# Five of 22 up-projection column pairs by seven block products, with one operand of the down-projection kept in DRAM meanwhile

## The chip, the cores and the metric

The kernel runs on one core of a Trainium2 chip. The metric is the device time of one launch in microseconds (us). TensorE (PE) multiplies, VectorE (DVE) and ScalarE (ACT) work elementwise, GpSimd (POOL) does small things, and SyncE (SP) issues nearly all DMAs. Each engine takes its instructions in the order in which they stand in its own list and stops at the first one whose inputs are not ready.

## The reference

One encoder block on 512 tokens of width 1024, in float32: two attention branches, then a gated feed-forward with a causal convolution of width 3 over the tokens. The change touches the feed-forward alone:

```python
def conv_glu(x, w_up, conv_w, conv_b, w_down):
    hid = x @ w_up                      # 512 x 1024 by 1024 x 5632
    hid = lax.conv_general_dilated(hid, ...) + conv_b
    gate, up = hid[..., :D_FF], hid[..., D_FF:]
    return (jax.nn.silu(gate) * up) @ w_down

x = x + conv_glu(rms_norm(x, norm2_g[l]), ...)
```

## The kernel before

**Products.** A float32 operand is split into hi and lo parts; every product is three matmuls (hi by hi, hi by lo, lo by hi). On the activations' side these are `hth` and `htl`, the transposed, normalised tokens (8 blocks of 128 features by 512 tokens).

**The up-projection.** The 5632 columns are worked through as 22 column pairs, up0 to up21: 128 gate columns and the 128 up columns that belong to them. A pair multiplies into two PSUM banks, `pg` and `pu`, with 8 blocks of features x 3 x 2 = 48 matmuls of 512 tokens. Only up0 and up1 run in halves of 256 tokens, since they start while the second half of the tokens is still being normalised.

**Around a pair.** `run_chunk` interleaves pair j with `split_gen` of pair j+1: ACT casts the raw weights to `whi`, DVE subtracts to get `wlo`, and SP then loads the raw weights of j+3 into the place that came free (1 MB a pair, two places). When `pg` is done, `conv` runs on it: one ACT activation for the last tap into `cg`, two DVE steps for the other taps, then SiLU on ACT. `pu` gets the same into `ub`, and DVE multiplies. `cg` has one place. `BANK` hands out PSUM banks in turn.

**For the down-projection,** which is done by seven block products already, `pair_sums` makes two operands from every second pair: `ax`, used in the first of its two sweeps, and `ay` (768 KB), used in the second. Before the change all eleven of each stay in SBUF.

**Order.** Nothing is queued dynamically: the order of each engine's list is fixed when the program is built, in part by the order of the Python generators and in part by the scheduler that merges them. The lists below are of the built programs.

Of the kernel before, what the change touches and what calls it, by code (L numbers as in the profile page):

```python
# [8 lines left out]
F32 = mybir.dt.float32  # L9
F32R = mybir.dt.float32r  # L10
AF = mybir.ActivationFunctionType
ALU = mybir.AluOpType
# [3 lines left out]
P = 128  # L16
# [42 lines left out]


CHUNKS = _chunks()


@with_exitstack
def block_kernel(ctx: ExitStack, tc: tile.TileContext, x, xt, params, g2, rbx, wts, wd0, wd1, out):
# [71 lines left out]
    def split_down(n, raw, hi, lo):  # L137
# [23 lines left out]
        else:  # L161
# [3 lines left out]
            yield  # L165
            part(0, raw[:, 0:1024])

    def split_gen(i, pieces):
# [6 lines left out]
        sh = 48 if key[:2] in ("qA", "kA", "vA", "vB") else 16 if key in ("up0", "up1") else 0  # L175
        n = 512 * kn if i >= FIRST_DN else 2048
        hi = wp.tile([P, 2112], F32R, tag="whi", name=f"whi_{key}")[:, sh:sh + n]
        lo = wp.tile([P, 2112], F32R, tag="wlo", name=f"wlo_{key}")[:, sh:sh + n]
        splits[key] = (hi.rearrange("p (k c) -> p k c", k=kn), lo.rearrange("p (k c) -> p k c", k=kn))
        if i >= FIRST_DN:  # L180
            yield from split_down(i - FIRST_DN, raw, hi, lo)
        n = 2048 // pieces
        for j in range(pieces if i < FIRST_DN else 0):
            sl = slice(n * j, n * (j + 1))
            if i == 0 and j == 0:
                V.tensor_copy(hi[:, sl], raw[:, sl])
            else:
                A.copy(hi[:, sl], raw[:, sl])  # L188
            E = G if i == 2 else V
            E.tensor_tensor(lo[:, sl], raw[:, sl], hi[:, sl].bitcast(F32), op=ALU.subtract)  # L190
            if j < pieces - 1:
                yield


        nxt = {0: None, 1: i + 3, 2: None}.get(i - FIRST_DN, i + 2)
        if nxt is not None and nxt < len(order):
            next(load(nxt))
        yield

    pos = {k: i for i, k in enumerate(order)}  # L200

    def run_chunk(key, body, pieces=4):

        sp = split_gen(pos[key] + 1, pieces)
        hi, lo = splits.pop(key)
        for _ in body(hi, lo):
            next(sp, None)
            yield
        for _ in sp:
            pass  # L210
# [11 lines left out]

    pp = ctx.enter_context(tc.tile_pool(name="pp", bufs=1, space=PSUM))
    dram = ctx.enter_context(tc.tile_pool(name="dram", bufs=1, space=bass.MemoryType.DRAM))


    reset = pool_c.tile([P, S], F32, tag="reset", name="reset")
# [35 lines left out]
    def norm_T(src, xn, gain, t, psum, nm):  # L263

        ss = pool_c.tile([P, 1], F32, tag="ss", name=f"ss_{nm}{t}", bufs=4)
        dump = pool_st.tile([P, D], F32, tag="skh", name=f"dump_{nm}{t}", bufs=2)
        A.activation(dump, src, AF.Square, accum_out=ss)
        rs = rstd_of(ss, 1, D, f"rs_{nm}{t}")
        for b in range(2):
            cs = slice(b * 512, (b + 1) * 512)  # L270
            V.scalar_tensor_tensor(xn[:, cs], src[:, cs], rs[:, 0:1], gain[b], op0=ALU.mult, op1=ALU.mult)
            ps = psum(f"tp_{nm}{t}{b}")
            for k in range(4):
                PE.transpose(ps[:, k * P:(k + 1) * P], xn[:, (4 * b + k) * P:(4 * b + k + 1) * P], ident)
            p3 = ps.rearrange("p (k q) -> p k q", k=4)
            hv = hth[:, 4 * b:4 * b + 4, t * P:(t + 1) * P]
            A.copy(hv, p3)
            V.tensor_tensor(htl[:, 4 * b:4 * b + 4, t * P:(t + 1) * P], p3, hv.bitcast(F32), op=ALU.subtract)

# [531 lines left out]
    def up_mm(ps, hi, lo, o, c0, c1):  # L811
        for k in range(NK):
            mm3(ps[:, c0:c1], hi[:, k, o:o + P], lo[:, k, o:o + P],
                hth[:, k, c0:c1], htl[:, k, c0:c1], k == 0, k == NK - 1)
            if k == 3:
                yield
        yield

    def gate(j, pg):
        g = fp.tile([P, S], F32, tag="cg", name=f"cg{j}", bufs=1)  # L820
        conv(pg, j, g)
        A.activation(g, g, AF.Silu)
        return g

    def pair_sums(i):

        u0, u1 = ub[:, 2 * i % 4, :], ub[:, 2 * i % 4 + 1, :]
        u = ub[:, 2 * i % 4:2 * i % 4 + 2, :].rearrange("p a b -> p (a b)")
        lo_, hi_ = slice(0, 256), slice(256, 512)
        t = {}  # L830
        if i < 8:
            ax = fp.tile([P, 2048], F32R, tag="ax", name=f"ax{i}", bufs=8)
            ay = fp.tile([P, 1536], F32R, tag="ay", name=f"ay{i}", bufs=8)
        else:

            pool = fp if i == 8 else late["hp"]
            ax = pool.tile([P, 2048], F32R, tag=f"ax{i}", name=f"ax{i}")
            ay = pool.tile([P, 1536], F32R, tag=f"ay{i}", name=f"ay{i}")
            if i == 8:
                keep[0] = fp.tile([P, S], F32, tag="t2", name="t2_0")  # L840
        pairs[i] = (ax, ay)

        def sums():
            t["st"] = st = fp.tile([P, 768], F32, tag="st", name=f"st{i}", bufs=1)
            s1, s42 = st[:, 0:256], st[:, 256:768]
            if i == 9:

                s42 = fp.tile([P, S], F32, tag="cg", name="s42_9", bufs=1)
            s4, s2 = s42[:, 0:256], s42[:, 256:512]
            t["s42"] = s42  # L850
            ins = [V.tensor_tensor(s1, u0[:, hi_], u1[:, hi_], op=ALU.add),
                   V.tensor_tensor(u0[:, hi_], u0[:, lo_], u0[:, hi_], op=ALU.subtract),
                   V.tensor_tensor(s2, s1, u0[:, lo_], op=ALU.subtract),
                   V.tensor_tensor(s4, u1[:, lo_], s2, op=ALU.subtract)]
            return ins

        def halves(a, parts):
            ins, n = [], a.shape[-1] // 2
            for o, src in parts:
                sl = slice(o, o + src.shape[-1])  # L860
                A.copy(a[:, sl], src)
                ins.append(V.tensor_tensor(a[:, n + o:n + sl.stop], src, a[:, sl].bitcast(F32), op=ALU.subtract))
# [13 lines left out]
    def up_fin(j, pg, pu, g=None):  # L876
        if g is None:
            g = gate(j, pg)
        u = ub[:, j % 4, :]
        conv(pu, NF + j, u)  # L880
        late["fin"] = (V.tensor_tensor(u, g, u, op=ALU.mult),)
        if j % 2 == 1 and j // 2 < 9:
            for step in pair_sums(j // 2):
                step()

    def up_body(j):
        def body(hi, lo):
            pg, pu = BANK(f"pg{j}", j - 1), BANK(f"pu{j}", j - 1)
            yield from up_mm(pg, hi, lo, 0, 0, S)
            g = gate(j, pg)  # L890
            yield from up_mm(pu, hi, lo, P, 0, S)
            up_fin(j, pg, pu, g)
        return body


# [2 lines left out]
    def up_first(j):  # L898
        def body(hi, lo):
            pg, pu = BANK(f"pg{j}", 0), BANK(f"pu{j}", 0)  # L900
            halves.append((hi, lo, pg, pu))
            yield from up_mm(pg, hi, lo, 0, 0, 256)
            yield from up_mm(pu, hi, lo, P, 0, 256)
            if j == 1:
                for i, (h, l, g, u) in enumerate(halves):
# [3 lines left out]
        return body  # L909

    for j in range(NF):
        for _ in run_chunk(f"up{j}", up_first(j) if j < 2 else up_body(j), pieces=4 if j < 2 else 2):
            pass

# [147 lines left out]
def _layout(inputs):  # L1062
# [12 lines left out]
    for i, (_, kn, parts) in enumerate(CHUNKS[:-2 * NP]):  # L1075
        views = [f[name][0][r0:r0 + kn * P, c0:c0 + n] for name, r0, c0, n in parts]
        w = views[0] if len(views) == 1 else np.concatenate(views, axis=1)
        wts[i] = w.reshape(kn, P, 2048 // kn).transpose(1, 0, 2).reshape(P, 2048)

    w = f["w_ffn_down"][0].reshape(NP, 2, P, 2, 512)  # L1080
# [20 lines left out]
```

## Time and profile before

| | us |
|---|---|
| median of 3 runs (lowest, highest) | 731.25 (730.97, 731.89) |
| profiled execution, and its span | 730.74, 729.0 |
| TensorE busy in the span | 723.3 |
| up2 starts | 401.70 |
| down-projection starts | 619.30 |
| DVE busy, ACT busy in the span | 533.8, 380.4 |

The span is what the profiler sees of the execution; 1.7 us lie around it. Times inside the program are counted from the span's start. In lines of the profile an instruction is named by its line, engine, output and inputs, with tile numbers left out; the first number is its start, the second its duration. Neighbouring instructions of one engine overlap, so that what one costs is read from start to start.

### The profile page before, as it was taken

The page shows a single profiled execution, that of the slowest core. Times are in us where ns is not written, and L with a number is a line of the kernel's source. Part 1 is how long each engine was busy: PE and PEld are TensorE (multiplying, and loading weights), DVE is VectorE, ACT ScalarE, POOL GpSimd, SP SyncE. Part 2 cuts the span into 40 slices and gives each one's busy share as a digit, 9 for nine tenths or more (in the row PEclk, how much of TensorE's full clock was granted, in tenths as well). Part 3 has the DMA queues.
Part 4 walks back from the last instruction along what each step waited for, and adds up shares of the span by engine and source line. Part 5 has one row for each costly group of instructions (what it writes and reads, how often), then busy time and mean ns, then how long its engine had stood idle before and what let it go on. Part 6 is the DMA issues. An engine that isn't in the chain of part 4 may idle for free.

```text
span 729.0 us, 10033 instructions
## 1 busy us (share of the span) xinstructions
PE 723.3 (99%) x3839; PEld 623.0 (85%) x3839; DVE 533.8 (73%) x967; ACT 380.4 (52%) x685; POOL 41.7 (6%) x73
## 2 busy tenths in 40 slices
PE   9999999999999999999999999999999999999997
PEld 8999998888988888888889888888888888888885
DVE  6678867775987888375275877667777675997686
ACT  6676556556856686343153553444554443543531
POOL 2701200000110111000000000000000000000000
PEclk9999999999999999999999999999999999999999
DMA  9632222121231112225342423223213313354563
GB/s 314 244 127 87 77 112 83 64 66 62 106 101 73 58 59 98 105 68 205 139 167 64 145 81 116 102 71 116 106 68 116 111 62 115 126 204 170 181 214 116
DMA packets 17905, 85.68 MB, mean 118 GB/s; under 512 B 2112, under 2 KB 2752, under 8 KB 10304
## 3 DMA queue, kind: packets, MB, share of 16 engines
q1 hardware_dynamic: 17568, 84.90, 32.5%
q8 instruction: 30, 0.49, 0.3%
q14 instruction: 19, 0.16, 0.1%
q10 hardware_dynamic: 288, 0.14, 0.1%
HBM read 80.84 MB, written 4.19 MB: 117 GB/s over the span
## 4 chain that ended last, share of the span: by engine, by line
PE 99%; DVE 0%; DVEq 0%; issue 0%
PE P L943 14%; PE pg L215 5%; PE pu L215 5%; PE pg L216 5%; PE pg L214 5%; PE pu L216 5%; PE pu L214 5%; PE qkB L216 2%; PE gB L216 2%; PE qkB L214 2%; PE gA L214 2%; PE gA L215 2%; PE gB L214 2%; PE gA L216 2%; PE qkB L215 2%; PE gB L215 2%
## 5 line engine op out<-in xcount | busy, mean ns | idle before, releaser
L190 DVE TENSOR_TENSOR wlo_up<-raw_up,whi_up 128x1024 fp32r<-128x1024 f32 (+1 forms) x50 | 52.4, 1093 | 47.1 <-ACT whi_up L188 47.1
L216 PE MATMUL pg<-hth,wlo_up 128*128 128x512 f32 (+1 forms) x192 | 71.2, 371 | 0.0
L215 PE MATMUL pu<-htl,whi_up 128*128 128x512 f32 (+1 forms) x192 | 71.2, 371 | 0.0
L214 PE MATMUL pg<-hth,whi_up 128*128 128x512 f32 (+1 forms) x192 | 71.2, 371 | 0.0
L214 PE MATMUL pu<-hth,whi_up 128*128 128x512 f32 (+1 forms) x192 | 71.2, 371 | 0.0
L215 PE MATMUL pg<-htl,whi_up 128*128 128x512 f32 (+1 forms) x192 | 71.1, 371 | 0.0
L216 PE MATMUL pu<-hth,wlo_up 128*128 128x512 f32 (+1 forms) x192 | 71.1, 370 | 0.0
L188 ACT CAST whi_up<-raw_up 128x1024 fp32r<-128x1024 f32 (+1 forms) x50 | 44.6, 948 | 27.2 <-PE pu L215 22.7
L943 PE MATMUL P<-whi_dn,ax 128*128 128x512 f32 x176 | 54.4, 389 | 0.0
L147 ACT CAST whi_dn<-raw_dn 128x1024 fp32r<-128x1024 f32 x33 | 34.3, 1052 | 27.9 <-PE P L943 19.9
L143 DVE TENSOR_TENSOR wlo_dn<-raw_dn,whi_dn 128x1024 fp32r<-128x1024 f32 x33 | 39.9, 1223 | 9.3 <-ACT whi_dn L147 9.3
L214 PEld LDWEIGHTS pu<-hth,whi_up 128*128 128x128 f32 x192 | 36.1, 188 | 6.3
L215 PEld LDWEIGHTS pg<-htl,whi_up 128*128 128x128 f32 x192 | 36.1, 188 | 6.2
L214 PEld LDWEIGHTS pg<-hth,whi_up 128*128 128x128 f32 x192 | 36.0, 188 | 6.3
L216 PEld LDWEIGHTS pg<-hth,wlo_up 128*128 128x128 f32 x192 | 36.1, 188 | 6.2
L216 PEld LDWEIGHTS pu<-hth,wlo_up 128*128 128x128 f32 x192 | 36.0, 188 | 6.2
L215 PEld LDWEIGHTS pu<-htl,whi_up 128*128 128x128 f32 x192 | 36.0, 188 | 6.2
L943 PE MATMUL P<-whi_dn,ay 128*128 128x512 f32 x132 | 40.8, 389 | 0.0
L943 PEld LDWEIGHTS P<-whi_dn,ax 128*128 128x128 f32 x176 | 33.0, 188 | 6.9
L806 ACT ACTIVATE cg<-pg,par 128x512 f32<-128x512 f32 x22 | 17.1, 778 | 39.4 <-PE pg L216 32.2
L943 PE MATMUL P<-wlo_dn,ax 128*128 128x512 f32 x88 | 34.2, 389 | 0.0
L588 DVE TENSOR_TENSOR_SCAN aB<-aB,reset 128x127 f32<-128x127 f32 (+3 forms) x32 | 26.0, 815 | 6.7 <-ACT aB L583 6.7
(250 smaller groups left out, 1970.2 us busy)
## 6 DMA issues: line engine op xcount, KB each, us to landing
raw_up<-in_wts SPq DMA_DIRECT2D x22, 1024.0 KB, 4.8
raw_dn<-in_wd SPq DMA_DIRECT2D x11, 1024.0 KB, 4.8
raw_dn<-in_wd SPq DMA_DIRECT2D x11, 512.0 KB, 3.3
raw_gA<-in_wts SPq DMA_DIRECT2D x4, 1024.0 KB, 4.8
raw_qkB<-in_wts SPq DMA_DIRECT2D x4, 1024.0 KB, 4.8
raw_gB<-in_wts SPq DMA_DIRECT2D x4, 1024.0 KB, 4.8
raw_wo<-in_wts SPq DMA_DIRECT2D x4, 1024.0 KB, 4.8
xs<-in_xt SPq DMA_DIRECT2D x8, 256.0 KB, 5.3
```

Source lines behind the costliest of these rows:

```text
L143: chain("halves", V.tensor_tensor(o, x, y, op=op))
L147: chain("casts", A.copy(hi[:, sl], src))
L188: A.copy(hi[:, sl], raw[:, sl])
L190: E.tensor_tensor(lo[:, sl], raw[:, sl], hi[:, sl].bitcast(F32), op=ALU.subtract)
L214: PE.matmul(ps, sh, mh, start=first, stop=False)
L215: PE.matmul(ps, sh, ml, start=False, stop=False)
L216: PE.matmul(ps, sl, mh, start=False, stop=last)
L588: V.tensor_tensor_scan(ar, ar, reset[:, S - n:S - 1][:, ::-1], 1.0, op0=ALU.mult, op1=ALU.max)
L806: tap = A.activation(c, ps, AF.Identity, scale=cw(2), bias=par[:, C_CB + tile_idx:C_CB + tile_idx + 1])
L943: chain("products", PE.matmul(dst, st, mv, start=first and n == 0, stop=last and n == 2, skip_group_check=True))
```

## The change

Pairs 5, 8, 11, 14 and 17 are computed as a 2 by 2 block product (features in two halves, tokens in two halves, and gate and up columns as the two halves of the columns) with seven products in the place of eight. Each of the seven is 4 feature blocks x 3 matmuls of 256 tokens, 84 matmuls in a pair.

- Four of the operands are sums of blocks of weights (`block_sums`, DVE, 512 columns each, on the raw weights of the next pair) with hi and lo parts of their own (`split_seven`: `wxh`, `wxl`).
- Four are sums of blocks of tokens, `ts1` to `ts4`, made once (`token_sums`). They need the transposed tokens in full float32: `norm_T` copies each transposed PSUM tile once more (`xf`, ACT) and GpSimd writes it to DRAM (`htd`, eight DMAs of 256 KB); after the last, eight DMAs on SP bring all of it back in runs of 512 bytes (`xT0`, `xT1`), and DVE and ACT make sums and parts during up0's second half to up3.
- The seven products go to four banks, `b1`, `b5`, `b7`, `b6`; `b1`, `b5` and `b7` take a second product on top of the first, once ACT has copied the first out (`pc`). DVE combines them into `hg` and `hu` in SBUF, which `conv` then reads where it read PSUM.
- To make room, `ay` has one place. GpSimd writes each of the first seven to DRAM (`ayd`) and fetches five back after up18 and two more in the first sweep.
- The host lays out the weights of the five pairs by blocks.

```diff
+SEVEN = (5, 8, 11, 14, 17)
...
+    def block_sums(i):
+        b = raws[i].rearrange("p (b c) -> p b c", c=512)
+        sx = late["pool"].tile([P, 1536], F32, tag="sx", name=f"sx_{order[i]}")
+        late["sx"] = sx
+        s1, s2, s4 = (sx[:, 512 * j:512 * (j + 1)] for j in range(3))
+        V.tensor_tensor(s1, b[:, 1], b[:, 3], op=ALU.add)
+        yield
+        V.tensor_tensor(s2, s1, b[:, 0], op=ALU.subtract)
+        yield
+        V.tensor_tensor(s4, b[:, 2], s2, op=ALU.subtract)
+        yield
+        V.tensor_tensor(b[:, 1], b[:, 0], b[:, 1], op=ALU.subtract)
+        yield
+    def split_seven(i, raw, hi, lo):
+        key = order[i]
+        wh, wl = (late["pool"].tile([P, 1600], F32R, tag=tag, name=f"{tag}_{key}")[:, 16:1552]
+                  for tag in ("wxh", "wxl"))
+        splits[key] = tuple(t.rearrange("p (k c) -> p k c", c=P) for t in (hi, lo, wh, wl))
+        sx = late["sx"]
+        for j, (h, l, src) in enumerate(((hi[:, 0:1024], lo[:, 0:1024], raw[:, 0:1024]),
+                                         (wh[:, 0:1024], wl[:, 0:1024], sx[:, 0:1024]),
+                                         (hi[:, 1024:2048], lo[:, 1024:2048], raw[:, 1024:2048]),
+                                         (wh[:, 1024:1536], wl[:, 1024:1536], sx[:, 1024:1536]))):
+            A.copy(h, src)
+            V.tensor_tensor(l, src, h.bitcast(F32), op=ALU.subtract)
+            if j < 3:
+                yield
...
+        if is_seven(i + 1):
+            yield from block_sums(i + 1)
...
+            xf = pool_wk.tile([P, S], F32, tag="wa", name=f"xf_{nm}{t}{b}", bufs=4)
+            A.copy(xf, ps)
+            G.dma_start(htd[t, b], xf)
...
-            ay = fp.tile([P, 1536], F32R, tag="ay", name=f"ay{i}", bufs=8)
+            ay = fp.tile([P, 1536], F32R, tag="ay", name=f"ay{i}")
...
+            if j // 2 < 7:
+                G.dma_start(ayd[j // 2], pairs[j // 2][1].bitcast(F32))
...
+            if j in (2, 3):
+                next(late["ts"])
...
+    def fetch(i):
+        tag = {0: "sx", 1: "wxl"}.get(i, "ts" if i < 5 else "ax")
+        n, bufs = {"sx": (1536, 1), "wxl": (1600, 1), "ts": (2048, 4), "ax": (2048, 8)}[tag]
+        ay = fp.tile([P, n], F32R, tag=tag, name=f"ay{i}", bufs=bufs)[:, 0:1536]
+        G.dma_start(ay, ayd[i])
+        pairs[i] = (pairs[i][0], ay)
+    ts = {}
+    def token_sums():
+        x = []
+        for i in range(2):
+            x.append(fp.tile([P, 2, 1024], F32, tag="ax", name=f"xT{i}", bufs=8))
+            for t in range(2):
+                for b in range(2):
+                    SP.dma_start(x[i][:, b].rearrange("p (k q) -> p k q", k=4)[:, :, t * P:(t + 1) * P],
+                                 htd[2 * i + t, b].rearrange("p (k q) -> p k q", k=4))
+        b11, b21, b12, b22 = x[0][:, 0], x[0][:, 1], x[1][:, 0], x[1][:, 1]
+        yield
+        V.tensor_tensor(b22, b22, b12, op=ALU.subtract)
+        yield
+        V.tensor_tensor(b12, b12, b11, op=ALU.subtract)
+        yield
+        V.tensor_tensor(b11, b22, b11, op=ALU.add)
+        yield
+        V.tensor_tensor(b21, b21, b11, op=ALU.subtract)
+        yield
+        for i, src in ((1, b12), (3, b22), (2, b11), (4, b21)):
+            t = fp.tile([P, 2, 1024], F32R, tag="ts", name=f"ts{i}", bufs=4)
+            A.copy(t[:, 0], src)
+            V.tensor_tensor(t[:, 1], src, t[:, 0].bitcast(F32), op=ALU.subtract)
+            ts[i] = [t[:, j].rearrange("p (k q) -> p k q", k=4) for j in range(2)]
+            yield
+    def up_seven(j):
+        def body(hi, lo, wh, wl):
+            b1, b5, b7, b6 = [BANK(f"p{n}_{j}", j - 1 + i // 2)[:, 0:256] for i, n in enumerate((1, 5, 7, 6))]
+            left, right = slice(0, 256), slice(256, 512)
+            pc = fp.tile([P, 3, 256], F32, tag="pc", name=f"pc{j}")
+            hg = fp.tile([P, S], F32, tag="hg", name=f"hg{j}")
+            hu = fp.tile([P, S], F32, tag="hu", name=f"hu{j}")
+            def prod(ps, w, b, h, first=True, last=True):
+                for k in range(4):
+                    sh, sl = w[0][:, 4 * b + k, :], w[1][:, 4 * b + k, :]
+                    for n, (st, mv) in enumerate(((sh, h[0]), (sh, h[1]), (sl, h[0]))):
+                        PE.matmul(ps, st, mv[:, k, :], start=first and k == 0 and n == 0,
+                                  stop=last and k == 3 and n == 2, skip_group_check=True)
+            r, w = (hi, lo), (wh, wl)
+            B = lambda a, q: [t[:, 4 * a:4 * a + 4, q] for t in (hth, htl)]
+            prod(b1, r, 0, B(0, left), last=False)
+            A.copy(pc[:, 0], b1)
+            yield
+            prod(b5, w, 0, ts[1], last=False)
+            A.copy(pc[:, 1], b5)
+            yield
+            prod(b7, r, 1, ts[3], last=False)
+            A.copy(pc[:, 2], b7)
+            V.tensor_tensor(pc[:, 1], pc[:, 1], pc[:, 2], op=ALU.add)
+            yield
+            prod(b6, w, 1, ts[2])
+            V.tensor_tensor(hu[:, right], b6, pc[:, 0], op=ALU.add)
+            yield
+            prod(b1, r, 2, B(1, left), first=False)
+            A.copy(hg[:, left], b1)
+            yield
+            prod(b5, w, 2, B(1, right), first=False)
+            V.tensor_tensor(hg[:, right], b5, hu[:, right], op=ALU.add)
+            g = gate(j, hg)
+            yield
+            prod(b7, r, 3, ts[4], first=False)
+            V.tensor_tensor(hu[:, left], b7, hu[:, right], op=ALU.add)
+            V.tensor_tensor(hu[:, right], hu[:, right], pc[:, 1], op=ALU.add)
+            up_fin(j, None, hu, g)
+            yield
         return body
...
-                    yield from up_mm(g, h, l, 0, 256, S)
-                    yield from up_mm(u, h, l, P, 256, S)
+                    for o, ps in ((0, g), (P, u)):
+                        for _ in up_mm(ps, h, l, o, 256, S):
+                            n += 1
+                            if n == 1 or 4 <= n < 8:
+                                next(late["ts"])
+                            yield
...
+        body = up_first(j) if j < 2 else up_seven(j) if j in SEVEN else up_body(j)
+        for _ in run_chunk(f"up{j}", body, pieces=4 if j < 2 else 2):
             pass
+        if j == 18:
+            for i in range(5):
+                fetch(i)
...
+            fetch(i - 4)
...
```

On DVE, from the convolution of `pu0` on (`L808`/`L809` before and `L853`/`L854` after are convolution steps with the coefficients `par`, `L190` and `L228` the lo part of weights, `L881` and `L928` the gating multiplication, `L851` the first of the sums `st` of `pair_sums`). Before:

```order
L808 SCALAR_TENSOR_TENSOR ub_4158<-pu0_4160,par_88,ub_4158 128x511
L809 SCALAR_TENSOR_TENSOR ub_4158<-pu0_4160,par_88,ub_4158 128x510
L881 TENSOR_TENSOR ub_4158<-cg0_4331,ub_4158 128x512
L190 TENSOR_TENSOR wlo_up3_4427<-raw_up3_4219,whi_up3_4426 128x1024 x2
L808 SCALAR_TENSOR_TENSOR ub_4158<-pu1_4222,par_88,ub_4158 128x511
L808 SCALAR_TENSOR_TENSOR cg1_4388<-pg1_4221,par_88,cg1_4388 128x511
L809 SCALAR_TENSOR_TENSOR ub_4158<-pu1_4222,par_88,ub_4158 128x510
L809 SCALAR_TENSOR_TENSOR cg1_4388<-pg1_4221,par_88,cg1_4388 128x510
L881 TENSOR_TENSOR ub_4158<-cg1_4388,ub_4158 128x512
L851 TENSOR_TENSOR st0_4399<-ub_4158 128x256
```

After:

```order
L853 SCALAR_TENSOR_TENSOR ub_4184<-pu0_4186,par_88,ub_4184 128x511
L854 SCALAR_TENSOR_TENSOR ub_4184<-pu0_4186,par_88,ub_4184 128x510
L971 TENSOR_TENSOR xT1_4326<-xT1_4326 128x1024
L928 TENSOR_TENSOR ub_4184<-cg0_4368,ub_4184 128x512
L228 TENSOR_TENSOR wlo_up3_4468<-raw_up3_4245,whi_up3_4467 128x1024
L973 TENSOR_TENSOR xT1_4326<-xT1_4326,xT0_4321 128x1024
L228 TENSOR_TENSOR wlo_up3_4468<-raw_up3_4245,whi_up3_4467 128x1024
L853 SCALAR_TENSOR_TENSOR ub_4184<-pu1_4248,par_88,ub_4184 128x511
L853 SCALAR_TENSOR_TENSOR cg1_4428<-pg1_4247,par_88,cg1_4428 128x511
L975 TENSOR_TENSOR xT0_4321<-xT1_4326,xT0_4321 128x1024
L982 TENSOR_TENSOR ts1_4492<-xT1_4326,ts1_4492 128x1024
L854 SCALAR_TENSOR_TENSOR ub_4184<-pu1_4248,par_88,ub_4184 128x510
```

The first token sum (`L971`) now stands between the convolution of `pu0` and the multiplication of pair 0, and the other sums and their lo parts (`L982`) between the split of up3 and the convolutions of up1.

On ACT, at the start of up5, where the weights of up6 are cast (`whi_up6`) and the tap of `pu4` is taken (`L806` and `L851` are taps, `L822` and `L867` the SiLU, `L861` and `L908` the casts of `pair_sums`). Before:

```order
L861 CAST ay1_4547<-st1_4548 128x512
L822 ACTIVATE cg4_4595<-cg4_4595 128x512
L188 CAST whi_up6_4642<-raw_up6_4511 128x1024 x2
L806 ACTIVATE ub_4158<-pu4_4562,par_88 128x512
L806 ACTIVATE cg5_4662<-pg5_4628,par_88 128x512
L822 ACTIVATE cg5_4662<-cg5_4662 128x512
L188 CAST whi_up7_4724<-raw_up7_4593 128x1024 x2
```

After:

```order
L867 ACTIVATE cg2_4487<-cg2_4487 128x512
L908 CAST ay0_4438<-st0_4439 128x512
L851 ACTIVATE cg3_4560<-pg3_4526,par_88 128x512
L226 CAST whi_up6_4713<-raw_up6_4558 128x1024 x2
L851 ACTIVATE ub_4184<-pu4_4621,par_88 128x512
L1003 COPY pc5_4697<-p1_5_4693 128x256
L1006 COPY pc5_4697<-p5_5_4694 128x256
L867 ACTIVATE cg3_4560<-cg3_4560 128x512
L1009 COPY pc5_4697<-p7_5_4695 128x256
```

The copies that release `p1`, `p5` and `p7` (`L1003`, `L1006`, `L1009`) stand behind the tap of pair 3's gate, the casts of up6 and the tap of `pu4`, in one queue.

On SP, from the loads of the weights of up2. Before:

```order
L130 DMA raw_up2_4114<-in_wts 128x2048
L761 DMA x2d_3790<-x2_3789 128x1024 x2
L130 DMA raw_up3_4219<-in_wts 128x2048
L130 DMA raw_up4_4281<-in_wts 128x2048
L130 DMA raw_up5_4444<-in_wts 128x2048
```

After:

```order
L132 DMA raw_up2_4134<-in_wts 128x2048
L806 DMA x2d_3792<-x2_3791 128x1024 x2
L132 DMA raw_up3_4245<-in_wts 128x2048
L967 DMA xT0_4321<-htd_107 128x4x128 x4
L967 DMA xT1_4326<-htd_107 128x4x128 x4
L132 DMA raw_up4_4307<-in_wts 128x2048
L132 DMA raw_up5_4485<-in_wts 128x2048
```

The eight reloads of the tokens stand ahead of the weights of up4.

More of the change, by code (lines that the diff above doesn't have):

```diff
@@ L166, in split_down, with is_seven @@
             part(0, raw[:, 0:1024])
+    def is_seven(i):
+        return i < len(order) and order[i] in [f"up{j}" for j in SEVEN]
+    def block_sums(i):
[25 more added lines that the diff above has]
+                yield
     def split_gen(i, pieces):
@@ L174, in split_gen @@
         raw = raws.pop(i)
-        sh = 48 if key[:2] in ("qA", "kA", "vA", "vB") else 16 if key in ("up0", "up1") else 0
+        sh = 48 if key[:2] in ("qA", "kA", "vA", "vB") else 16 if key in ("up0", "up1") or is_seven(i) else 0
         n = 512 * kn if i >= FIRST_DN else 2048
@@ L181, in split_gen @@
             yield from split_down(i - FIRST_DN, raw, hi, lo)
+        elif is_seven(i):
+            yield from split_seven(i, raw, hi, lo)
         n = 2048 // pieces
-        for j in range(pieces if i < FIRST_DN else 0):
+        for j in range(pieces if i < FIRST_DN and not is_seven(i) else 0):
             sl = slice(n * j, n * (j + 1))
@@ L204, in run_chunk @@
         sp = split_gen(pos[key] + 1, pieces)
-        hi, lo = splits.pop(key)
-        for _ in body(hi, lo):
+        for _ in body(*splits.pop(key)):
             next(sp, None)
@@ L832, in pair_sums @@
             ax = fp.tile([P, 2048], F32R, tag="ax", name=f"ax{i}", bufs=8)
-            ay = fp.tile([P, 1536], F32R, tag="ay", name=f"ay{i}", bufs=8)
-        else:
[L836 to L840, printed above, removed]
+            ay = fp.tile([P, 1536], F32R, tag="ay", name=f"ay{i}")
+        elif i == 8:
+            ax = fp.tile([P, 2048], F32R, tag="ts", name=f"ax{i}", bufs=4)
+            ay = fp.tile([P, 1600], F32R, tag="wxh", name=f"ay{i}")[:, 0:1536]
+            keep[0] = fp.tile([P, S], F32, tag="hg", name="t2_0")
+        else:
+            ax = late["hp"].tile([P, 2048], F32R, tag=f"ax{i}", name=f"ax{i}")
+            ay = late["hp"].tile([P, 1536], F32R, tag=f"ay{i}", name=f"ay{i}")
         pairs[i] = (ax, ay)
@@ L1074, in _layout @@
     wts = np.empty((len(CHUNKS) - 2 * NP, P, 2048), np.float32)
-    for i, (_, kn, parts) in enumerate(CHUNKS[:-2 * NP]):
+    for i, (key, kn, parts) in enumerate(CHUNKS[:-2 * NP]):
         views = [f[name][0][r0:r0 + kn * P, c0:c0 + n] for name, r0, c0, n in parts]
         w = views[0] if len(views) == 1 else np.concatenate(views, axis=1)
+        if key in [f"up{j}" for j in SEVEN]:
+            a = w.reshape(2, 4, P, 2, P).transpose(0, 3, 2, 1, 4)
+            wts[i] = np.concatenate([a[k, f].reshape(P, 512) for k in range(2) for f in range(2)], axis=1)
+            continue
         wts[i] = w.reshape(kn, P, 2048 // kn).transpose(1, 0, 2).reshape(P, 2048)
```

8 lines of the change are left out of this document (7 added, 1 removed).

## The prediction

> **What bounds the kernel now.** I read the page first: busy time, the clock, the chain.
>
> ```profile
> PE 723.3 (99%) x3839; PEld 623.0 (85%) x3839; DVE 533.8 (73%) x967; ACT 380.4 (52%) x685; POOL 41.7 (6%) x73
> PEclk9999999999999999999999999999999999999999
> PE 99%; DVE 0%; DVEq 0%; issue 0%
> ```
>
> TensorE is busy 99% of the span at an ungated clock and is 99% of the chain that ended last. Time can be won only by giving TensorE less to do, and is lost wherever it is made to wait. Next the windows of the up-projection: up2 to up21, then up2 to up4, then up5 alone.
>
> ```profile
> 401.70:619.30 217.60, 217.60 (x962) 180.17 (x961) 155.19 (x220) 100.58 (x138) 0.00 (x0) 1.00 0.28 101
> 401.70:434.30 32.60, 32.60 (x146) 27.00 (x145) 26.43 (x40) 17.30 (x25) 0.00 (x0) 1.00 0.35 125
> 434.30:445.20 10.90, 10.90 (x49) 9.02 (x49) 5.96 (x7) 4.09 (x5) 0.00 (x0) 1.00 0.27 96
> ```
>
> The columns after the length are busy us (count) of TensorE, its weight loads, VectorE (DVE), ScalarE (ACT) and GpSimd, then clock, DMA share, GB/s. The 20 pairs take 217.60 us with no TensorE gap, so 10.88 us each. DVE has 155.19/20 = 7.76 us of work in a pair, ACT 5.0. DVE is the second engine; the change loads it most.
>
> **What TensorE gains.** A seven-product pair runs 7 x 4 x 3 = 84 matmuls of 256 columns for 48 of 512. The wide ones start 10.88/48 = 0.2267 us apart. The narrow shape, from the timeline of TensorE in up0 and up1, which are done in halves of 256 tokens:
>
> ```profile
> 379.04 0.28 PE L214 MATMUL pg<-hth,whi_up 128*128 128x256 f32 x1
> ...
> 383.40 0.28 PE L216 MATMUL pu<-hth,wlo_up 128*128 128x256 f32 x1
> ...
> 384.77 0.28 PE L214 MATMUL pg<-hth,whi_up 128*128 128x256 f32 x1
> ...
> 386.37 0.28 PE L216 MATMUL pg<-hth,wlo_up 128*128 128x256 f32 x1
> ```
>
> From 379.04 to 383.40 there are 37 steps, 0.1178 us each; from 384.77 to 386.37 there are 14, 0.1143 each. By these, 84 cost 9.60 to 9.90 us. I take 0.1145 (nearer the later stretch, half a wide one): 9.62, which saves 1.26 us a pair and **6.3 us** for five. The ends are 4.9 and 6.4. Break-even is 10.88/84 = 0.1295.
>
> The Trainium skill, "TensorE: Matmul & The Clock Gate", section Back-to-back issue gap, speaks against the change: load-and-multiply streams run at about 81 ns at 128 columns and 131 at 512. Halfway on that line, an estimate from the page, 256 columns cost 98, so 84 would cost 1.31 times 48 wide ones, and the total would be some 17 us worse instead of 6.3 better. The rows above (0.1145 against 0.2267, half) disagree with the page.
>
> **What DVE gains.** Its prices are start-to-start times of one tight stretch:
>
> ```profile
> 446.29 2.36 DVE L190 TENSOR_TENSOR wlo_up<-raw_up,whi_up 128x1024 fp32r<-128x1024 f32 x2 [3.89 <-ACT whi_up L188]
> 448.56 0.74 DVE L808 SCALAR_TENSOR_TENSOR ub<-pu,par,ub 128x511 f32<-128x511 f32 x1
> ...
> 451.29 0.42 DVE L862 TENSOR_TENSOR ay<-ub,ay 128x256 fp32r<-128x256 f32 x1
> 451.63 0.42 DVE L852 TENSOR_TENSOR ub<-ub 128x256 f32<-128x256 f32 x1
> 451.97 0.42 DVE L853 TENSOR_TENSOR st<-st,ub 128x256 f32<-128x256 f32 x1
> ...
> 453.63 0.95 DVE L862 TENSOR_TENSOR ax<-ub,ax 128x768 fp32r<-128x768 f32 x1
> 454.50 0.74 DVE L809 SCALAR_TENSOR_TENSOR cg<-pg,par,cg 128x510 f32<-128x510 f32 x1
> 455.16 0.68 DVE L862 TENSOR_TENSOR ay<-st,ay 128x512 fp32r<-128x512 f32 x1
> 397.21 2.50 DVE L190 TENSOR_TENSOR wlo_up<-raw_up,whi_up 128x512 fp32r<-128x512 f32 x4 [0.67 <-ACT whi_up L188]
> ```
>
> 1024 columns 1.14 us (448.56 - 446.29, halved), 768 0.87, a conv step 0.66, 512 0.61 (2.50/4, less the overlap of the last), 256 0.34. Where one reads the result before it, it takes up to 0.1 more; priced so, this stretch adds up to 9.2 us against 9.5 measured, so chains get a factor 1.03.
>
> Per seven-product pair DVE gets four block sums of 512 (2.44), the lo parts of the sums (1.14 + 0.61) and five combinations of 256 (1.70): 5.9 us. Three pairs, one of them by seven, hold 3 x 7.76 + 5.9 = 29.2 us of DVE work in 2 x 10.88 + 9.62 = 31.4 us of TensorE: 93%. It fits, with 2.2 us to spare, but no longer pair by pair: lag is carried. ACT gets a cast of 1024 and of 512 and four copies of 256 (0.95 + 0.5 + 4 x 0.3 = 2.7): 7.7 of 9.6, covered, unless it waits behind DVE.
>
> **The token sums, once.** DVE does four sums and four lo parts of 1024: 8 x 1.14 = 9.1 us in up0's tail to up4. up2 to up4 have 32.6 - 26.4 = 6.2 us free; with up5's first sums (2.44 + 1.14 + 0.61 = 4.2) 13.3 come in, so DVE enters up5 some 7 us behind. Worse, the first sum stands in DVE's order right after up0's conv and waits for all eight reloads of the transposed activations, and wlo of up3, the convs and wlo of up4 are queued behind it. When do those reloads land? Rows for that:
>
> ```profile
> 377.70 1.06 ACT L267 ACTIVATE dump_n<-x 128x1024 f32<-128x1024 f32 x1 [2.69 <-issue]
> 394.19 0.78 ACT L806 ACTIVATE cg<-pg,par 128x512 f32<-128x512 f32 x1 [4.66 <-PE pg L216]
> 388.88 1.37 DVE L278 TENSOR_TENSOR htl<-tp_n,hth 128x512 fp32r<-128x512 f32 x2 [2.32 <-ACT hth L277]
> 401.54 0.69 DVE L881 TENSOR_TENSOR ub<-cg,ub 128x512 f32<-128x512 f32 x1
> 374.06 0.33 SPq L130 DMA_DIRECT2D raw_up<-in_wts  x1
> raw_up<-in_wts SPq DMA_DIRECT2D x22, 1024.0 KB, 4.8
> out<-x SPq DMA_DIRECT2D x7, 256.0 KB, 2.1
> xs<-in_xt SPq DMA_DIRECT2D x8, 256.0 KB, 5.3
> GB/s 314 244 127 87 77 112 83 64 66 62 106 101 73 58 59 98 105 68 205 139 167 64 145 81 116 102 71 116 106 68 116 111 62 115 126 204 170 181 214 116
> ```
>
> The last extra PSUM copies follow the htl of 390.25: two of 0.67 us, so 391.5 (ACT is idle up to 394.19, and for 2.69 us ahead of 377.70, where four of the eight fit: free). A 256 KB write lands in 2.1 us from SP; from GpSimd, which issues none in the trace of before, I take that to twice that: 393.6 to 396. Then SP issues eight loads, 2.1 MB; at the first slice's 314 GB/s that is 6.7 us, plus about 2 for the first to land: 402.5 to 404.5. Their 512-byte runs have no row here; at half that rate 410. I take 405.5, near the fast end, since loads of 256 KB land in 5.3 us under full load. DVE would have been free at 402.2. On SP the eight issues (0.33 each) end at 398.6 at the latest, ahead of raw_up4, which waits for the wlo of up2 until 399.7 anyhow and has 12.9 us for its 4.8: free.
>
> The Trainium skill, "DMA: Bandwidth & Descriptors", section Why small descriptors are slow (HBM only), charges about 3 cycles a packet on top of one per 32 bytes: 19 for 16 at 512 bytes. By that estimate 6.7 us become 7.9 and the forecast below rises by 1.2; no run here shows it.
>
> From there the chain runs, by the changed order: 39 DVE instructions from the first sum to the multiplication of pair 2 that frees cg (15 of 1024, 8 of 512, 9 conv steps, 6 of 256, one of 768: 30.8, by 1.03 31.8 us), then on ACT the tap of pair 3's gate, two casts of up6, the tap of pair 4 (rows below: 0.67 + 1.9 + 0.67) and the first copy of up5's products (0.3), 3.5 us: T + 35.3, T being the landing of the reloads.
>
> ```profile
> 403.67 0.78 ACT L806 ACTIVATE ub<-pu,par 128x512 f32<-128x512 f32 x1
> 404.34 0.77 ACT L806 ACTIVATE cg<-pg,par 128x512 f32<-128x512 f32 x1
> 445.20 2.00 ACT L188 CAST whi_up<-raw_up 128x1024 fp32r<-128x1024 f32 x2 [2.07 <-PE pu L215]
> 447.10 0.77 ACT L806 ACTIVATE ub<-pu,par 128x512 f32<-128x512 f32 x1
> 451.84 0.39 ACT L861 CAST ax<-st 128x256 fp32r<-128x256 f32 x1
> ```
>
> TensorE wants that copy, which releases b1 for its second sum, at 434.34 + 48 x 0.1145 = 439.84. So it stops in the middle of up5 for T - 404.5 us: **1.0 us** at T = 405.5, nothing up to 404.5, 5.5 at 410. What is late next: the same copy in up8 and up11, while the lag is worked off 2.2 us a period; I put 0.5 us for both (0 to 2).
>
> **The rest.** GpSimd writes and refetches seven ay operands (768 KB each). Nothing else is on its queue in the up-projection (0.00 in the windows) and the DMA share is 0.28. The one ay tile is rewritten first some 7 us after it is full (ay1's first cast in up5, by the same walk), against an estimate of 5 us for the write, from the 4.8 of raw_up: hidden, and if not, DVE waits for the difference. The refetches start in up18, with 40 us and more to their use. In norm 2 the scale of token group 2 is queued on GpSimd behind four issues:
>
> ```profile
> 379.12 0.55 POOL L100 TENSOR_TENSOR rs_n<-rs_n,nhalf 128x1 f32<-128x1 f32 x1 [11.01 <-DVE rs_n L99]
> 383.53 0.60 PE L274 MATMUL tp_n<-ident,xn 128*128 128x128 f32 x4
> ```
>
> Its last copy is ready at 377.7. [...] The down-projection's order stays.
>
> **Sum.** 6.3 - 1.0 - 0.5 = 4.8 us off the profiled 730.74, which is 0.5 below the median 731.25: 726.5. Ends: 6.4 without a stall gives 724.9 (DVE chains without the factor, faster reloads); 4.9 - 5.5 - 2, everything at its worst, 733.9.
>
> **Rivals.**
> Late reloads (T = 408 to 411) or DVE chains 6% longer than priced: the stall in up5 is 4 to 6 us, the gain mostly eaten: 728.5 to 732. For it: the unseen GpSimd issue and 512-byte runs. Against it: DMA share 0.3.
> DVE becomes the bound, the slower side: place, every seven-product pair; it decides from 3 x 10.88 = 32.6 us of DVE work in three pairs, 12% over my 29.2. At 15% the five periods last 33.6, 0.95 too much each: 4.8 us plus the 1.5 of stalls, 737.5. For it: 93% leaves little for hand-offs between in-order queues. Against it: SBUF-only forms (L852, L853) cost as the rest per column.
> 256 columns cost more than half of 512, through the weight loads that stand in the same number before half the columns: slower from 0.1295; at 0.135 a pair takes 11.34 us, five lose 2.3, 733.6 before any stall. The rows of 0.1143 and 0.1178, with a load for each matmul too, speak against.
> It does nothing: what TensorE saves returns as the same wait for the copies in every one of the five pairs, 1.26 us each: 731.2. For it, that each of the seven products hands over in 1.4 us; against it, that other pairs have DVE idle (5.96 of 10.9).
>
> **How the numbers follow.** Forecast 0.62 (its own range 724.5 to 728.5); late reloads 0.19, of which faster 0.11, same 0.05, slower 0.03; DVE bound 0.09; narrow matmuls 0.03; nothing gained 0.03; and 0.04 that the gain is larger. A measurement of this kernel tells 0.2%, 1.5 us, from no change. Faster 0.77, same 0.08, slower 0.15. The range 724.4 to 732 leaves out the slower rivals and a bit below.
>
> **What would show it.** Right: 84 matmuls of 256 columns 0.114 to 0.118 us apart in up5, up8, up11, up14, up17; one TensorE gap of 0.5 to 2 us in up5 before the second sum on b1, released by ACT's copy; DVE busy over 90% from 405 to 570; down-projection starting at 614.5 instead of 619.3. Wrong: gaps in up3 or up4 (reloads landing after 408), gaps of over 1 us in each seven-product pair (DVE bound), a step over 0.125.

## The result: 5.2 us faster

The changed kernel takes 726.36 us (726.17 to 726.66, 4 runs) against 731.57 of the kernel before on the same chip; ratio 0.9932, interval 0.9919 to 0.9945. The forecast was 726.5.

The page of the changed kernel, busy time, clock and chain:

```profile
PE 718.6 (99%) x4019; PEld 627.5 (87%) x4019; DVE 565.4 (78%) x1030; ACT 401.5 (55%) x727; POOL 53.6 (7%) x95
PEclk9999999999999999999999999999999999999999
PE 98%; DMA 1%; SPq 0%; DVE 0%; ACT 0%; DVEq 0%; issue 0%
```

TensorE is still the bound, with 4.7 us less to do; DVE has 31.6 us more, ACT 21. The windows of the changed kernel, columns as in the prediction: up2 to up21, up2 to up4, up5, up6 and up7, and what follows.

```profile
402.77:615.62 212.85, 212.85 (x1142) 184.68 (x1141) 188.08 (x283) 117.18 (x172) 6.45 (x12) 1.00 0.43 151
402.77:435.44 32.67, 32.67 (x147) 27.04 (x146) 29.38 (x38) 17.73 (x23) 0.00 (x0) 1.00 0.36 120
435.44:445.33 9.89, 9.89 (x86) 9.89 (x84) 9.89 (x16) 6.96 (x13) 0.54 (x1) 1.00 0.67 261
445.33:467.12 21.79, 21.79 (x99) 18.03 (x98) 21.79 (x37) 13.05 (x19) 0.53 (x1) 1.00 0.38 140
615.62:724.90 109.28, 105.09 (x463) 86.47 (x461) 89.27 (x116) 45.90 (x57) 1.07 (x2) 1.00 0.52 183
```

From the start of up2 to that of the down-projection it is 212.85 us, 4.78 less than the 217.63 of before (619.31 - 401.68 by the same matmuls), and TensorE has no gap in it. A seven-product pair takes 9.89 us, 0.99 less than 10.88. From up5 to up7 DVE is busy without a pause, for 31.7 us. Behind the start of the down-projection the two profiles differ by 0.4 us, all of it behind the last matmul, where the last write lands.

Single profiles cannot be compared by their spans: TensorE waits 0 to 2.2 us for the first weights, by an amount that differs from profile to profile.

```profile
7.61 0.74 PE L379 MATMUL qA<-whi_qA,hth 128*128 128x256 f32 x4 [0.59 <-ACT whi_qA L226]
```

This is the changed kernel's; with 0.37 us ahead of it, it makes most of the 1.09 us by which up2 starts later than in the profile of before, which waited for nothing there. So the experiments are compared by the stretch from up2 to the down-projection, next to the times.

### The profile page after: what moved, and what is told of

Its sections match the earlier page's. It is cut to its first block, busy times and chain, and to the rows that moved or that the text cites. A ratio compares the mean times of both kernels' runs of the same rounds, so it can differ in the third digit from the quotient of the medians.

```text
span 724.9 us, 10589 instructions
## 1 busy us (share of the span) xinstructions
PE 718.6 (99%) x4019; PEld 627.5 (87%) x4019; DVE 565.4 (78%) x1030; ACT 401.5 (55%) x727; POOL 53.6 (7%) x95
## 4 chain that ended last, share of the span: by engine, by line
PE 98%; DMA 1%; SPq 0%; DVE 0%; ACT 0%; DVEq 0%; issue 0%
PE P L1087 14%; PE p L998 7%; PE pg L254 4%; PE pg L253 4%; PE pg L255 4%; PE pu L254 4%; PE pu L255 4%; PE pu L253 4%; PE qkB L255 2%; PE gB L255 2%; PE qkB L253 2%; PE gA L253 2%; PE gA L254 2%; PE gB L253 2%; PE gA L255 2%; PE qkB L254 2%
## 5 line engine op out<-in xcount | busy, mean ns | idle before, releaser
L253 PE MATMUL pg<-hth,whi_up 128*128 128x512 f32 (+1 forms) x152 | 55.7, 367 | 0.0
L255 PE MATMUL pg<-hth,wlo_up 128*128 128x512 f32 (+1 forms) x152 | 55.7, 366 | 0.0
L254 PE MATMUL pg<-htl,whi_up 128*128 128x512 f32 (+1 forms) x152 | 55.7, 366 | 0.0
L254 PE MATMUL pu<-htl,whi_up 128*128 128x512 f32 (+1 forms) x152 | 55.6, 366 | 0.0
L253 PE MATMUL pu<-hth,whi_up 128*128 128x512 f32 (+1 forms) x152 | 55.6, 366 | 0.0
L255 PE MATMUL pu<-hth,wlo_up 128*128 128x512 f32 (+1 forms) x152 | 55.6, 365 | 0.0
L228 DVE TENSOR_TENSOR wlo_up<-raw_up,whi_up 128x1024 fp32r<-128x1024 f32 (+1 forms) x40 | 41.2, 1062 | 7.0 <-ACT whi_up L226 7.0
L226 ACT CAST whi_up<-raw_up 128x1024 fp32r<-128x1024 f32 (+1 forms) x40 | 34.5, 917 | 14.7 <-PE pu L254 7.9
L253 PEld LDWEIGHTS pu<-hth,whi_up 128*128 128x128 f32 x152 | 28.5, 188 | 4.7
L1087 PEld LDWEIGHTS P<-whi_dn,ay 128*128 128x128 f32 x132 | 24.8, 188 | 5.1
```

The costliest lines, as they stand in the source:

```text
L253: PE.matmul(ps, sh, mh, start=first, stop=False)
L254: PE.matmul(ps, sh, ml, start=False, stop=False)
L255: PE.matmul(ps, sl, mh, start=False, stop=last)
L1087: chain("products", PE.matmul(dst, st, mv, start=first and n == 0, stop=last and n == 2, skip_group_check=True))
```

## The experiments

| kernel | up2 to down-projection, us | median, us | ratio to before (interval) |
|---|---|---|---|
| before | 217.63 | 731.05 to 731.57 | |
| changed, five pairs | 212.85 | 726.36 | 0.9932 (0.9919 to 0.9945) |
| e1, four extra matmuls a pair | 213.47 | 728.22 | 0.9957 (0.9944 to 0.9971) |
| e2, reloads twice | 213.69 | 727.52, one run | |
| e3, no pair by seven | 217.63 | 730.78 | 0.9992 (0.9983 to 1.0001) |
| e4, seven pairs | 213.13 | 728.41 | 0.9966 (0.9953 to 0.9978) |
| e5, one extra matmul a pair | 212.00 | 725.64 | 0.9924 (0.9909 to 0.9939) |
| e6, two matmuls in halves | 212.39 | 726.23 | 0.9933 (0.9916 to 0.9949) |
| e7, up4 for up5 | 216.33 | 730.01, one run | |
| e8, six pairs, one extra each | 210.43 | 724.86 | 0.9921 (0.9908 to 0.9935) |
| e9, as e5, again | 212.00 | 725.27 | 0.9921 (0.9909 to 0.9933) |
| e10, changed, again | 212.86 | 726.06 | 0.9930 (0.9918 to 0.9943) |

**e3, the overhead alone.** `SEVEN = ()`.

> No pair by seven products; everything else of the change stays: the extra PSUM copies, the way of the tokens through DRAM and back, the token sums (then unused), ay by way of DRAM. Theory A (all of that is hidden): the time of before, 731.3 within 0.5. Theory B (it costs about a microsecond that the pairs' gain hides): 732.3 or more.

The stretch is 217.63 us, to the hundredth that of before, with 8.3 us more on DVE (163.49 for 155.19) and twelve GpSimd DMAs in it:

```profile
402.82:620.45 217.63, 217.63 (x963) 180.25 (x961) 163.49 (x228) 104.13 (x142) 6.44 (x12) 1.00 0.41 147
```

Theory A: copies, detours through DRAM and token sums cost nothing that these runs resolve (the interval of the ratio ends at 1.0001). The whole change of the stretch lies in the five pairs. Their block sums and combinations are not in e3.

**e1, what sets the step of 0.1178 us.** Ahead of the first product:

```diff
+            for n in range(4):
+                PE.matmul(full[0][:, 256:384], hi[:, 0, :], hth[:, 0, 0:128], start=True, stop=True,
+                          skip_group_check=True)
```

> Four extra matmuls of 128 columns at the head of each seven-product pair, into columns of a PSUM bank that nobody reads. In the changed kernel the 256-column matmuls of these pairs start 0.1178 us apart; in up1 and in the second halves of up0 and up1 it was 0.1134, after narrower transposes had come in between, and with the same weight place, PSUM bank and activations as up5. Theory A (the step depends on what TensorE ran just before: a stream that comes straight out of 512-column matmuls keeps the slower step until something narrow interrupts it): 0.1134 after the four, each pair 9.53 plus about 0.4, time about 726.4 - 5 x (0.37 - 0.4) = 726.4 or a few tenths either way, and the step visible in the profile. Theory B (the step belongs to the operands or to how the pairs are written): 0.1178 stays, time 728.2 or so.

The step became 0.1133. Three places of TensorE's timeline in e1: the start of up5, and, in up11, the point at which the scheduler had put nine 512-column matmuls of the next pair between two products.

```profile
435.94 0.56 PE L991 MATMUL p<-hth,whi_up 128*128 128x128 f32 x4
436.33 0.33 PE L1002 MATMUL p<-hth,whi_up 128*128 128x256 f32 x1
436.51 0.28 PE L1002 MATMUL p<-htl,whi_up 128*128 128x256 f32 x1
...
437.66 0.28 PE L1002 MATMUL p<-hth,wlo_up 128*128 128x256 f32 x1
...
507.24 0.39 PE L255 MATMUL pg<-hth,wlo_up 128*128 128x512 f32 x1
507.46 0.28 PE L1002 MATMUL p<-hth,whi_up 128*128 128x256 f32 x1
...
508.88 0.28 PE L1002 MATMUL p<-hth,wxh_up 128*128 128x256 f32 x1
```

From 436.51 to 437.66 are ten steps, 0.115 with the first ones, and 0.1133 over the next microseconds; from 507.46 to 508.88, behind the wide ones, twelve steps of 0.118. Same pair, same weights, same banks: theory A, the step is a state of the stream that wide matmuls leave behind and narrower ones end. The four cost 0.39 us a pair and bring 0.30, not the 0.37 expected, since the first steps behind them are longer. So such a pair takes 9.99 us instead of 9.89, up11 with its wide matmuls loses more, and the stretch is longer (213.47). The median, 728.22, is the one that theory B named; the steps decide for A all the same. It rose by 1.9 us, of which the stretch has 0.6; 0.5 stands ahead of up2 in the profile, and where the rest lies is open.

**e5 and e6, how little is enough.** e5 has `range(1)` for `range(4)`. e6 does the first two matmuls of a pair as two halves of 128 columns (its start flags discard part of the first product, so it computes something else with the same work):

```diff
-                        PE.matmul(ps, st, mv[:, k, :], start=..., stop=..., ...)
+                        for c in ((0, 128), (128, 256)) if ps is b1 and first and k == 0 and n < 2 else ((0, 256),):
+                            PE.matmul(ps[:, c[0]:c[1]], st, mv[:, k, c[0]:c[1]], start=..., stop=..., ...)
```

> One extra matmul of 128 columns at the head of each seven-product pair in the place of four. Four brought the step of the 256-column matmuls from 0.1178 to 0.1134 us and cost 0.4 us a pair, so that the pair took 9.99 us for 9.89. Theory A1 (any single narrower matmul breaks the slow step): step 0.1134, pair 9.53 + about 0.1 = 9.6, five pairs 1.3 us less between up2 and the down-projection than in the changed kernel (212.85), 211.5. Theory A2 (it takes several in a row, or a stop): 0.1178 stays, pair 10.0, 213.3.

> No extra columns: the first two matmuls of each seven-product pair are done as two halves of 128 columns each. Theory A1 (narrower matmuls of any kind break the slow step): step 0.1134, pair 9.53 + about 0.2 = 9.7, up2 to the down-projection 212.0. Theory A2 (it has to be something outside of the accumulation, on another place of PSUM): 0.1178 and 213.5.

The first matmuls of up5 and the first of up6, in the changed kernel and then in e5:

```profile
435.21 0.39 PE L255 MATMUL pu<-hth,wlo_up 128*128 128x512 f32 x1
435.44 0.28 PE L998 MATMUL p<-hth,whi_up 128*128 128x256 f32 x1
...
445.33 0.40 PE L253 MATMUL pg<-hth,whi_up 128*128 128x512 f32 x1
```

```profile
434.96 0.22 PE L991 MATMUL p<-hth,whi_up 128*128 128x128 f32 x1
435.02 0.33 PE L1002 MATMUL p<-hth,whi_up 128*128 128x256 f32 x1
435.19 0.28 PE L1002 MATMUL p<-htl,whi_up 128*128 128x256 f32 x1
435.31 0.28 PE L1002 MATMUL p<-hth,wlo_up 128*128 128x256 f32 x1
...
444.62 0.40 PE L253 MATMUL pg<-hth,whi_up 128*128 128x512 f32 x1
```

One matmul of 128 columns costs 0.06 us and the pair falls from 9.89 to 9.66, its price included; halves bring it to 9.76. Theory A1 in both. The stretch is 212.00 rather than the 211.5 expected: in up11 and up17 wide matmuls stand between the products and the slow step comes back (0.19 us in each), and the pair behind each of the five is 0.03 longer.

**e2, later reloads.** The eight reloads are issued twice.

> All reloads of the transposed tokens are done twice, the second over the first, so the first token sum can start only when the second set has landed, some 6 to 9 us later than 406.1. Theory A (the chain of the prediction: landing + 34.4 us, as the changed kernel's trace has it, against the second sum of up5 at 441.1, margin 0.66 us): TensorE stands still in up3 to up5 for the delay less 0.7, about 5 to 8 us, time 731.5 to 735. Theory B (DVE has slack in up2 to up5 that takes up the delay): less than 2 us, time under 728.5.

The first token sum started at 416.58 rather than 406.06, but the stretch grew by 0.84 us only; TensorE's one longer stop is in up5, for a lo part:

```profile
437.05 0.39 PE L999 MATMUL p<-ts,wxl_up 128*128 128x256 f32 x1 [0.48 <-DVE wxl_up L200]
```

This is not the test that was meant: the program was built with the sums further down in DVE's order (12 instructions that stood behind the first sum now stand ahead of it), so that the chain of the prediction was another. Theory A's 5 to 8 us are wrong for this kernel. The time fits theory B, but it does not show slack in the changed kernel: the chain of the unchanged order stays untested here.

**e7, a pair earlier.** `SEVEN = (4, 8, 11, 14, 17)`.

> The first seven-product pair is up4 in the place of up5; still five pairs. DVE comes out of the token sums late: in the changed kernel it finishes the last of the sums and parts for up5 at 434.9, 0.5 us before up5 starts. Theory A (the margin of the prediction: DVE's lag after the token sums is what keeps up5 just free of stops): one pair earlier, 10.9 us of TensorE time are missing and 7.8 of DVE work with them, so TensorE stops about 3 us in up4 (2 to 5), up2 to the down-projection about 216. Theory B (DVE has several us to spare there): less than 1 us, under 213.9.

216.33 us, 3.5 above the changed kernel. TensorE stops in up4 and at its end, at three places that wait for DVE, one of them through ACT's queue (the rows name 2.5 us as idle; much of the rest is the longer steps around the stops):

```profile
408.01 1.23 DVE L971 TENSOR_TENSOR xT<-xT 128x1024 f32<-128x1024 f32 x1 [5.54 <-DMA xT<-htd]
425.61 0.28 PE L998 MATMUL p<-ts,wxl_up 128*128 128x256 f32 x1
...
426.41 0.28 PE L998 MATMUL p<-ts,whi_up 128*128 128x256 f32 x1
428.07 0.38 PE L998 MATMUL p<-hth,wlo_up 128*128 128x256 f32 x1 [1.39 <-DVE wlo_up L200]
428.29 0.28 PE L998 MATMUL p<-hth,whi_up 128*128 128x256 f32 x1
...
429.47 0.28 PE L998 MATMUL p<-ts,wlo_up 128*128 128x256 f32 x1
...
432.62 0.38 PE L998 MATMUL p<-hth,wxh_up 128*128 128x256 f32 x1 [0.40 <-ACT pc L1006]
437.66 0.50 PE L253 MATMUL pg<-hth,whi_up 128*128 128x512 f32 x1 [0.67 <-DVE hu L1013]
424.43:437.66 13.23, 10.69 (x86) 9.89 (x84) 13.23 (x21) 7.13 (x14) 0.00 (x0) 1.00 0.32 105
```

The last line is the window of up4: DVE busy for all of its 13.23 us. Theory A: DVE's lag after the token sums is real, and the changed kernel's first pair stands where it just does not reach TensorE. Two limits go with it. The reloads of this one run landed 2.1 us later than in the changed kernel, counted from the start of up2 (408.01 - 402.65 against 406.06 - 402.77), so a part of the 3.5 us may be theirs. And the longest stop is for a lo part; only the second goes through ACT's copies, the path of the prediction.

**e4 and e8, more pairs.** e4: `SEVEN = (5, 7, 9, 11, 13, 15, 17)`. e8: `SEVEN = (5, 8, 10, 12, 14, 17)` with the one extra matmul.

> Seven pairs by seven products in the place of five, every second one from up5 to up17. Two pairs then hold 2 x 7.76 + 5.9 = 21.4 us of DVE work in 10.88 + 9.89 = 20.8 us of TensorE. Theory A (DVE becomes the bound, the slower rival of the prediction): gaps of TensorE in the seven-product pairs that grow from pair to pair, 3 to 4 us in all against 2.0 gained: 727.5 to 728.5, slower than with five. Theory B (DVE still keeps up): 724.4, 0.99 us a pair.

> Six pairs by seven products (5, 8, 10, 12, 14, 17), each with the one extra matmul of 128 columns. TensorE would need 217.63 - 6 x 1.22 = 210.3 us between up2 and the down-projection. Theory A (DVE is the next bound as soon as seven-product pairs stand two apart: 21.4 us of DVE work in 10.88 + 9.66 = 20.5): three such periods cost about 0.9 each, less what the three-pair periods give back: 1 to 2 us of stops, 211.3 to 212.3, no better than five pairs (212.0). Theory B: no stops, 210.4, time about 724.2.

e4 stops TensorE twice, first for DVE's sum that frees p6's bank, later for a cast on ACT:

```profile
448.06 0.50 PE L253 MATMUL pg<-hth,whi_up 128*128 128x512 f32 x1 [0.42 <-DVE hu L1013]
549.62 0.68 DVE L183 TENSOR_TENSOR sx_up<-raw_up,sx_up 128x512 f32<-128x512 f32 x1
550.84 2.00 ACT L199 CAST whi_up<-raw_up 128x1024 fp32r<-128x1024 f32 x2 [3.17 <-PE p L998]
553.83 0.50 PE L998 MATMUL p<-ts,wxh_up 128*128 128x256 f32 x2 [1.26 <-ACT wxh_up L199]
437.58:566.26 128.68, 126.99 (x808) 115.23 (x807) 124.76 (x201) 76.52 (x122) 3.77 (x7) 1.00 0.41 148
479.88:500.68 20.80, 20.80 (x134) 18.91 (x133) 19.91 (x34) 12.62 (x21) 0.54 (x1) 1.00 0.39 139
```

Seven pairs at 9.89 would give 210.9 (with 0.03 for each change of step behind); 213.13 were measured: 2.2 us of stops, 0.7 at the first and 1.5 at the second. Only the first is theory A's. At the second the last block sum of up17 had ended at 550.30, and ACT had stood idle for 3.17 us until TensorE was done with the weights in whose place those of up17 go: the scheduler had put 14 of up17's 84 matmuls ahead of up16's wide ones, straight behind up15. Without that stop the stretch would be 211.6 by an estimate from these figures, 1.2 us shorter than with five pairs. In up9 and up10 (the last line) DVE has 19.91 us of work in 20.80, so it is close to the bound but not the bound. That the median, 728.41, lies in theory A's range is luck; the gaps that grow from pair to pair did not come.

e8 has no stop at all; its whole stretch, up8 to up17 alone, and in it up10 and up11, then up12 and up13:

```profile
403.37:613.80 210.43, 210.43 (x1185) 184.12 (x1183) 192.45 (x294) 120.02 (x178) 6.45 (x12) 1.00 0.42 153
467.48:570.25 102.77, 102.77 (x666) 93.34 (x665) 97.68 (x159) 62.42 (x99) 4.02 (x8) 1.00 0.41 149
488.04:508.60 20.56, 20.56 (x135) 18.67 (x134) 20.53 (x34) 12.68 (x21) 0.53 (x1) 1.00 0.38 141
508.60:529.15 20.55, 20.55 (x135) 18.71 (x134) 19.54 (x33) 11.89 (x19) 0.53 (x1) 1.00 0.38 141
```

TensorE is busy throughout, with DVE at 95%: theory B. My sum of 21.4 us of DVE work in two pairs was too high: in up12 and up13, the third such period, DVE has 19.54 us of work in 20.55 and is idle for the rest, so nothing piles up. The stretch is 1.57 us shorter than with five pairs and the extra matmul (e5, e9), 1.22 of it for the sixth pair. Its median of 724.86 us is the best of all, 1.2 below the changed kernel on the same chip (e10), e9's 0.8; but one of its five runs took 727.15, and its ratio to before is that of e9, so the times alone do not yet show that six pairs beat five.

## Why the prediction was right, and what was off in it

**The pairs' gain** was put at 6.3 us (step 0.1145) with ends of 4.9 and 6.4; it is 4.95 (five times 0.99). The term was mis-sized by choosing the wrong of two stretches of before: I took the step of up1 (0.1143), and the pairs run at that of up0 (0.1178). e1, e5 and e6 show why: up0's first half comes straight out of 512-column matmuls, as the pairs do, and up1's came behind transposes. Even 0.1143 is a mixture, of first steps near 0.118 and of later ones of 0.1134. Out of context, "nearer the later stretch" was a guess.

**The stop in up5** was put at 1.0 us and did not come. Its steps, in the changed kernel:

```profile
406.06 1.23 DVE L971 TENSOR_TENSOR xT<-xT 128x1024 f32<-128x1024 f32 x1 [3.47 <-DMA xT<-htd]
436.10 0.69 DVE L928 TENSOR_TENSOR ub<-cg,ub 128x512 f32<-128x512 f32 x1
436.83 0.78 ACT L851 ACTIVATE cg<-pg,par 128x512 f32<-128x512 f32 x1 [0.85 <-DVE ub L928]
439.39 0.78 ACT L851 ACTIVATE ub<-pu,par 128x512 f32<-128x512 f32 x1
440.06 0.37 ACT L1003 COPY pc<-p 128x256 f32<-128x256 f32 x1
```

The reloads landed at 406.06, which is 404.97 on the clock of before (1.09 earlier), against 405.5 forecast. The 39 DVE instructions took 30.77 us: the bare 30.8, not 31.8; nothing had to be added for results read at once. The factor came from a stretch in which the two conv steps on one tile follow each other, 0.78 us apart; in the changed kernel the scheduler has put other work between them, which is the likely reason. (By its own prices that stretch adds up to about 9.1 us, not 9.2.) The copy ended at 440.43, 34.4 us after the landing (35.3 forecast), and TensorE asks for it at 435.44 + 48 x 0.1177 = 441.09. So 0.66 us were left, of which 0.16 come from the slower step itself. DVE's lag does reach TensorE one pair earlier (e7), so the mechanism is there; the margin in up5 is on the other side of zero. Of the signs that the prediction named, the step (0.1178), DVE above 90% from 405 to 570 (153.38 us of 165) and the start of the down-projection (614.5 on the clock of before) came; the gap in up5 did not.

**The later stops** (0.5) did not come either: TensorE has no idle row in up8 and up11. DVE's price was too high as well: the stretch has 188.08 us of DVE work, e3's 163.49, so 4.9 us for each of the five pairs, not 5.9.

**The sum** of 4.8 was met (4.78) because the overrated gain and the stops that failed to come cancel: 6.3 - 1.5 for 4.95 - 0.17, the last being 0.03 us by which the pair behind each of the five is longer. The way, less multiplying for an engine that is the bound, is as told; that the forecast came within 0.2 us is luck, with two errors of about 1.4 us against each other.

**What was costed at nothing** cost nothing (e3), though not each step went as told. SP took 6.33 us for the eight issues, not 8 x 0.33, so raw_up4 went out at 401.6, 0.8 after the wlo of up2, with 12 us to its use. The scale of token group 2 was ready 1.6 us late by the same clock (GpSimd's issues of these writes took 0.54 to 0.75 us each), and the transposes went 0.7 late, with matmuls of up1 in between. The ay writes landed in 5.2 us. Rows on the DMAs:

```profile
395.16 6.33 SPq L967 DMA_DIRECT2D xT<-htd  x8
ayd<-ay POOLq DMA_DIRECT2D x7, 768.0 KB, 5.2
htd<-xf_n POOLq DMA_DIRECT2D x8, 256.0 KB, 3.3
xT<-htd SPq DMA_DIRECT2D x8, 256.0 KB, 5.2
397.50:401.59 4.09, 4.09 (x38) 4.09 (x38) 3.15 (x6) 3.38 (x6) 0.00 (x0) 1.00 0.99 258
```

The last line is a window of the reloads, up to the load of raw_up4 that follows them: 258 GB/s in runs of 512 bytes with the DMA engines full, 18% under the first slice's 314. The Trainium skill, "DMA: Bandwidth & Descriptors", section Why small descriptors are slow (HBM only), gives 16 parts in 19, 264 by an estimate from the page: the trace agrees, with a little more loss.

**The rivals.** Narrow matmuls above half the price: 0.1178 or 0.1134 against 0.2267 is 0.52 or 0.50 here. By the two sustained figures of the Trainium skill ("TensorE: Matmul & The Clock Gate", section Back-to-back issue gap) it would be 0.75, an estimate from the page; the trace does not agree. (The prediction's "halfway" is a third of the way from 128 to 512 columns; its 98 ns is right for that.) DVE as the bound: not with five pairs or six; with seven it costs 0.7 us once and is at 97%, and whether it would be the bound in another order is open. Late reloads: the landing was near the forecast. Nothing gained: TensorE has no gap in the stretch, so nothing of what it saves returns as a wait.

## What to carry to other kernels

A product with fewer multiplications is worth what its narrower matmuls cost at the place where they will run; read their step behind the same neighbours, and try one narrow matmul at the head of each group. What the sums add belongs on the second engine's clock over several groups, not one: here it was 100% busy for 30 us without TensorE noticing, and the group that had to come first was the one with almost nothing to spare (0.66 us). When an edit delays an input, look at the built order before reading its time; a scheduler may have moved the users. The same holds for a stop: in e4 the longer one came from the order and not from the engine that was nearly full.

## What the runs showed of the hardware that was not expected

TensorE's step for 256 columns has two values, 0.1178 us after 512-column matmuls and 0.1134 after matmuls of 128 columns, at a granted clock of 1.00 throughout, and keeps the one or the other for as long as the stream runs without a break (84 matmuls in the changed kernel, 9.6 us in e5). One matmul of 128 columns is enough to change it, within about four steps; it costs 0.06 us, and the pair is 0.23 us shorter with it.

Breaks of the stream change the step as well, and in the six that these traces have, it goes by their length from one start to the next. Behind 0.25 and 0.76 us (e2, at 438.54 and 436.29) and behind 0.36 and 0.68 us (e7, at 424.79 and 431.94) the step is 0.1134. Behind 1.55 us (e4, at 552.29) and 1.67 us (e7, at 426.41) it is 0.1178. The last is in the rows of e7: 0.114 from 425.61 to 426.41, and 0.118 from 428.29 to 429.47, with no wide matmul between. So wide matmuls are one way into the slower step and not the only one. Each break is from one execution, none lies between 0.76 and 1.55 us, and what in the engine holds the state, no run here shows.
